# A hybrid attention and SwiGLU layer on one Trainium2 core: the last activation chunk transposed on TensorE, the first norm's Newton steps on VectorE, and masks given two more steps

## The chip, the cores and the metric

The program runs on one core of a Trainium2 chip. A core has TensorE (PE in the profile, its weight loads PEld), VectorE (DVE), ScalarE (ACT), GpSimd (POOL) and SyncE (SP, which here only issues transfers), and 16 DMA engines that all queues share. Each engine runs its own instructions in their written order and waits on semaphores for the others. The metric is the device time of one execution in microseconds. The time before is 1340.16 us, the median of three runs: 1338.07, 1340.16 and 1351.09.

## The reference

One layer over 256 positions of width 2048. Two matrices carry most of the weight traffic: the input projection (2048 x 12288) and the feed-forward pair (2048 x 11264 and 5632 x 2048). Cut to what matters here:

```python
def hybrid_layer(x, ...):
    h = rmsnorm(x, g_mix)                       # first norm
    proj = h @ w_in                             # q, k, v of 16 heads, and three gates of 2048
    gates = sigmoid(proj[..., 3 * MIX_WIDTH:])
    o_a = stick_breaking_attention(q, k, v)     # heads 0 to 3: masked, no softmax
    o_b = moba_attention(rmsnorm(q), rmsnorm(k), v, rel_bias)
    o_c = dilated_attention(rmsnorm(q), rmsnorm(k), v, rel_bias)
    merged = gates[0] * (o_a @ w_b[a]) + gates[1] * (o_b @ w_b[b]) + gates[2] * (o_c @ w_b[c])
    x = x + merged @ w_out
    gu = rmsnorm(x, g_ffn) @ w_gu               # second norm, then gate and up, 5632 columns each
    return x + (silu(gu[..., :D_FF]) * gu[..., D_FF:]) @ w_down
```

Stick-breaking attention weighs a key by exp(log sigmoid(z) + the sum of log sigmoid(-z) over the keys after it), and masks both factors to keys strictly before the query.

## The kernel before

**Tiling.** Every matmul is a 128 x 128 stationary block of weights times 512 moving columns. For accuracy each f32 operand is split in two f32r parts: ScalarE copies the high part (`w_hi`), VectorE subtracts it for the low part (`w_lo`), both on line 110 (`split`), and lines 181 to 183 (`product`) issue three matmuls: high by high, low by high, high by low. A pair of weight blocks (`[P, 2, 512]`, 512 KB) is fetched by SP, split in one ScalarE and one VectorE instruction of 128 x 1024, and then used by twelve matmuls in most places. Wide products use one level of Strassen's scheme on some chunks (`form`, `sums`), which saves matmuls and adds VectorE sums (`u`, L325, L336, L1152 to L1167).

**Stages.** First the input projection, unit by unit (`units`: v, gate, q and k, ...), with the attention of the finished heads woven in; then the branch products, the output product, the second norm, the gate-and-up product in eleven chunks of 512 columns (loop over `c`, L1047), and the down projection in two halves of 1024 columns (`down_pair`).

**What sets the order.** The program is written as generators that are advanced one step per weight pair: `stages` at each, `slow_stages` at every second (L310 to L318). A `yield` thus puts what follows one step later. `behind(n, step)` runs a step after the n-th split. From this a scheduler with a timeline of its own then fixes the order on each engine; instructions marked `keep_in_program_order` keep theirs. So a `yield` more or an instruction on another engine moves neighbours too.

**First norm.** The sum of squares (`sst`, L518) goes through `rsqrt_mean`: one multiply-add (L188), Ln and Exp on ScalarE (L190, L191), and two Newton steps of four small instructions each (L194 to L197), on GpSimd here. The result `rstd` scales the projection's rows, so it is applied when the accumulation banks are read: L786 copies the two banks of `v` (named `ps`), L772 the two of the first gate (named `qs`). The products that come next, of q and k, write into the same two `ps` banks.

**Masks.** `stick_breaking` handles two heads at a time. GpSimd masks the softplus values (`pT`, L559) and later the weights (`p`, L559); then come three `yield`s and the product with `v` (L652, L653).

**Activations.** After each of the eleven gate-and-up chunks ScalarE and VectorE form 2 x 128 x 512 activations `sg[t]` (L1053, L1054). They are needed transposed, with the feature on the partition. Each half `t` is turned by `turn_out` (a ScalarE copy of the 16-bit halves, L705, and a DMA transpose from ScalarE's queue, L707) and `turn_in` (a ScalarE copy back, L712), written to `a_mem` in HBM (L1040), and fetched again in the down projection (`fetch_a`, L1065; `take_a`), where it is split. Three chunks stay in the core (`EARLY`). The last chunk, c = 10, uses as room the two tiles that will later hold its own split (`a_hi`, `a_lo`), is turned while the down projection already runs, and is used last. The down projection also fetches weights through SP (L302, and L107 where the order is pinned); its third weight quarter `b21` (a `g_raw` tile) feeds the sum L1167.

Of the kernel before, what the change touches and what calls it, by code (L numbers as in the profile page):

```python
# [13 lines left out]
ALU = mybir.AluOpType  # L14
# [5 lines left out]
D = 2048  # L20
S = 256
NT = S // P
# [8 lines left out]
EPS = 1e-6  # L31
# [26 lines left out]
def hybrid_block(ctx: ExitStack, tc: tile.TileContext, x, rel_bias, w_in, w_branch, w_out, w_gu, w_down, xT, gains,  # L58
                 onehot, extra, out):
    nc = tc.nc  # L60
# [22 lines left out]
    def pool(stack, name, side, bufs=1):  # L83
        return stack.enter_context(tc.tile_pool(name=name, bufs=bufs, side=side, reuse_waits="tile"))
# [8 lines left out]
    def half_kb(dt=F32):  # L93

        return scratch.tile([P, NB], dt, name="sc")
# [23 lines left out]
    split_count = [0]  # L119
# [7 lines left out]
    def behind(n, step, *args):  # L127
        at_split.setdefault(n, []).append(lambda: step(*args))
# [53 lines left out]
        nc.tensor.matmul(ps, ah, wl, start=False, stop=False, **how)  # L182
        nc.tensor.matmul(ps, al, wh, start=False, stop=stop, **how)  # L183

    def rsqrt_mean(dst, ss, n, cols, engine=nc.vector):

        v = small.tile([P, cols], F32, name=f"rs_v{cols}")
        engine.tensor_scalar(v, ss, 1.0 / n, EPS, op0=ALU.mult, op1=ALU.add)  # L188
        y = small.tile([P, cols], F32, name=f"rs_y{cols}")
        nc.scalar.activation(y, v, AF.Ln)  # L190
        nc.scalar.activation(y, y, AF.Exp, scale=-0.5)  # L191
        t = small.tile([P, cols], F32, name=f"rs_t{cols}")
        for it in range(2):
            engine.tensor_mul(t, y, y)  # L194
            engine.tensor_mul(t, t, v)
            engine.tensor_scalar(t, t, -0.5, 1.5, op0=ALU.mult, op1=ALU.add)
            engine.tensor_mul(dst if it else y, y, t)  # L197

    def transpose4(src):

        pt = tr.tile([P, 4, P], F32, name="tr")
        for i in range(4):
            nc.tensor.transpose(pt[:, i, :], src[:, i * P:(i + 1) * P], ident)
        return pt
# [232 lines left out]
    def squares(xc, dst, c):  # L437
        for t in range(NT):
            nc.scalar.activation(half_kb(), xc[t], AF.Square, accum_out=dst[:, t, c:c + 1])

    ss1 = small.tile([P, NT, 4], F32, name="ss1", bufs=1)
    rstd = small.tile([P, NT], F32, name="rstd", bufs=1)
# [70 lines left out]
    def first_norm():  # L513
        for c in range(3, 4):
            squares(rows[c], ss1, c)
            yield
        sst = small.tile([P, NT], F32, name="sst", bufs=1)
        nc.vector.tensor_reduce(sst, ss1, op=ALU.add, axis=AX.X)  # L518
        rsqrt_mean(rstd, sst, D, NT, nc.gpsimd)
        yield  # L520

    rest = [rest_of_x()]
# [19 lines left out]
    def sums_of_h():  # L542
        yield
        yield
        for c in WC:
# [6 lines left out]
            yield  # L552

    stages.extend((*rest, first_norm()))
    slow_stages.append(sums_of_h())


    def keep_before(blk):
        nc.gpsimd.affine_select(out=blk, in_=blk, compare_op=ALU.is_gt, fill=0.0, base=0,  # L559
                                pattern=[[0, 2], [1, P]], channel_multiplier=-1)  # L560
# [42 lines left out]
    def diag_blocks(a):  # L603
        return (a[:, 0:W0].rearrange("p (h q) -> p h q", h=2)[:, :, 0:P],
                a[:, W0:W0 + W1].rearrange("p (h q) -> p h q", h=2))

    def finish(h0, po):
        nc.scalar.copy(o_raw[:, h0:h0 + 2, :], po)

    def stick_breaking(hl, qT, kT, v):  # L610
        z = att.tile([P, 2 * NB], F32, name="att")
        for i in range(2):
            nc.tensor.matmul(z[:, i * S:(i + 1) * S], kT[:, hl + i, 0:P], qT[:, hl + i, :], start=True, stop=True)
        for i in range(2):
            nc.tensor.matmul(z[:, W0 + i * P:W0 + (i + 1) * P], kT[:, hl + i, P:S], qT[:, hl + i, P:S],
                             start=True, stop=True)
        n = W0 + W1
        l = pa.tile([P, n], F32, name="p", bufs=1)
        nc.scalar.activation(l, z[:, :n], AF.Abs)
        nc.scalar.activation(l, l, AF.Exp, scale=-1.0)  # L620
        nc.scalar.activation(l, l, AF.Ln, bias=1.0)
        sp = pa.tile([P, n], F32, name="pT", bufs=1)
        sp_hi = pa.tile([P, n], F32R, name="sp_hi", bufs=1)
        lo = half_kb(F32R), pa.tile([P, W1], F32R, name="sp_lo", bufs=1)
        nc.vector.scalar_tensor_tensor(sp, z[:, :n], 0.0, l, op0=ALU.max, op1=ALU.add)
        lb = l
        nc.vector.scalar_tensor_tensor(lb, z[:, :n], 0.0, l, op0=ALU.min, op1=ALU.subtract)
        for blk in diag_blocks(sp):
            keep_before(blk)
        nc.scalar.copy(sp_hi, sp)  # L630
        for part, cols in zip(lo, (slice(0, W0), slice(W0, n))):
            nc.vector.tensor_sub(part, sp[:, cols], sp_hi[:, cols].bitcast(F32))
        yield
        yield
        yield
        c = att.tile([P, 2 * NB], F32, name="att")
        late = c[:, 0:W0].rearrange("p (h q) -> p h q", h=2)[:, :, P:S]
        for i, (early, part) in enumerate(((sp_hi[:, 0:W0], sp_hi[:, W0:n]), lo)):
            nc.tensor.matmul(c[:, 0:W0], neg_after, early, start=not i, stop=False, skip_group_check=True)
            nc.tensor.matmul(late, neg_ones, part.rearrange("p (h q) -> p h q", h=2), start=False, stop=bool(i), skip_group_check=True)  # L640
            nc.tensor.matmul(c[:, W0:n], neg_after, part, start=not i, stop=bool(i), skip_group_check=True)
        nc.vector.tensor_add(lb, lb, c[:, :n])
        nc.scalar.activation(lb, lb, AF.Exp)
        for blk in diag_blocks(lb):
            keep_before(blk)
        yield
        yield
        yield
        po = tr.tile([P, 2, S], F32, name="tr")
        for i in range(2):  # L650
            cols = slice((hl + i) * HD, (hl + i + 1) * HD)
            nc.tensor.matmul(po[:, i, :], v[:, 0, cols], lb[:, i * S:(i + 1) * S], start=True, stop=False)  # L652
            nc.tensor.matmul(po[:, i, P:S], v[:, 1, cols], lb[:, W0 + i * P:W0 + (i + 1) * P],  # L653
                             start=False, stop=True)
        finish(hl, po)
# [297 lines left out]
    def out_of_rows(src, rooms, pl, name, bufs):  # L953

        rooms.append(pl.tile([P, 2, NB], F32, name=name, bufs=bufs).rearrange("p k n -> p (k n)"))
        turn_out(src, rooms[-1])
# [38 lines left out]
    for c in range(4):  # L995
# [4 lines left out]
        if c == 0:  # L1000
# [3 lines left out]
            ORDER = [0, 1, 2, 4, 3, 6, 5, 8, 7, 9, 10]  # L1004
            EARLY = 3
            a = Chunks(None, "a", NF // 4, WD, False)
# [35 lines left out]
    def to_a(c, srcs, out_at, in_at, room):  # L1042
        n, rooms = split_count[0], []
        for t in range(NT):
            behind(n + out_at[t], lambda t: out_of_rows(srcs[t], rooms, *room(t)), t)
            behind(n + in_at[t], into_a, c, t, rooms)

    for c in range(D_FF // NB):
        nxt = (h2, w_gu, (c + 1) * NB, D_FF + (c + 1) * NB, True) if c + 1 < D_FF // NB else None
        (g0, g1_, u0, u1), ahead = project_pair(h2, w_gu, c * NB, D_FF + c * NB, ahead, nxt)  # L1050
        sg = [half_kb() for _ in range(NT)]
        for t, (g, u) in enumerate(((g0, u0), (g1_, u1))):
            nc.scalar.activation(sg[t], g, AF.Silu, scale=rstd2[:, t:t + 1])  # L1053
            nc.vector.scalar_tensor_tensor(sg[t], u, rstd2[:, t:t + 1], sg[t], op0=ALU.mult, op1=ALU.mult)  # L1054
        if c < 9:
            to_a(c, sg, (14, 18), (PAIR + 3, PAIR + 7), lambda t: (pr, "a_raw", 2))
        elif c == 9:
            to_a(c, sg, (6, 10), (14, 18), lambda t: (gd, "g_raw", 4))
        else:
            to_a(c, sg, (5, 9), (14, 18), lambda t: (pd, ("a_hi10", "a_lo10")[t], 1))  # L1060


    def fetch_a(c):
        raw = pr.tile([P, 2, NB], F32, name="a_raw", bufs=2).rearrange("p k (j q) -> p (k j) q", j=2)
        nc.sync.dma_start(raw, a_mem[c])  # L1065
        return raw
# [12 lines left out]
    pd = pool(ctx, "pd", "left")  # L1079

    def take_rest():
        cs = ORDER[EARLY:]
        raws = [fetch_a(c) for c in cs[:2]]
        for i, (c, steps) in enumerate(zip(cs, (4, 6, 5, 6, 6, 6, 7, 7))):
            for _ in range(steps):
                yield
            take_a(pd, c, raws.pop(0))
            if i + 2 < len(cs) - 1:
                raws.append(fetch_a(cs[i + 2]))
            elif i + 2 == len(cs):  # L1090
                for _ in range(0):
                    yield
                raws.append(fetch_a(cs[-1]))

    stages.append(take_rest())

    def more_sums(cs, rooms):
# [157 lines left out]
```

## Time and profile before

| | |
|---|---|
| Times of three runs | 1338.07, 1340.16, 1351.09 us |
| Profiled execution | 1350.9 us, its span 1349.2 us, mean granted clock 0.996 |
| PE / DVE / ACT / POOL busy | 1331.0 / 1202.8 / 945.5 / 58.8 us |
| HBM read, written | 303.66 MB, 12.60 MB |

Busy times are sums over instructions; PE's is modelled and full in almost every slice, so what counts is where it is not full, and where the clock that TensorE was granted is below 1.00. A row of the timeline gives start, length, engine, line, operation and tile names, and in brackets the idle time of that engine just before and who ended it. Line numbers are those of the kernel before.

### The profile page before, as it was taken

The page shows a single profiled execution, that of the slowest core. Times are in us where ns is not written, and L with a number is a line of the kernel's source. Part 1 is how long each engine was busy: PE and PEld are TensorE (multiplying, and loading weights), DVE is VectorE, ACT ScalarE, POOL GpSimd, SP SyncE. Part 2 cuts the span into 40 slices and gives each one's busy share as a digit, 9 for nine tenths or more (in the row PEclk, how much of TensorE's full clock was granted, in tenths as well). Part 3 has the DMA queues.
Part 4 walks back from the last instruction along what each step waited for, and adds up shares of the span by engine and source line. Part 5 has one row for each costly group of instructions (what it writes and reads, how often), then busy time and mean ns, then how long its engine had stood idle before and what let it go on. Part 6 is the DMA issues. An engine that isn't in the chain of part 4 may idle for free.

```text
span 1349.2 us, 17457 instructions
## 1 busy us (share of the span) xinstructions
PE 1331.0 (99%) x6194; PEld 1155.8 (86%) x6194; DVE 1202.8 (89%) x1272; ACT 945.5 (70%) x1209; POOL 58.8 (4%) x74
## 2 busy tenths in 40 slices
PE   9999999999999999999999999999999999899998
PEld 7788888888888888888878888888888888788887
DVE  6998998989889987774889999999999998799998
ACT  7777787788766766665757778787777776564563
POOL 0301100000110100000000000000000000000000
PEclk9999999999999999999999999999999999899999
DMA  9995768677888867999976767678878789878663
GB/s 349 302 286 167 232 194 254 218 235 206 259 253 250 280 184 249 284 274 205 272 252 235 240 207 239 209 218 263 261 243 257 237 249 238 297 256 274 223 216 107
DMA packets 206391, 326.33 MB, mean 242 GB/s; under 512 B 46776, under 2 KB 58576, under 8 KB 206304
## 3 DMA queue, kind: packets, MB, share of 16 engines
q1 hardware_dynamic: 151632, 291.54, 64.9%
q0 software_dynamic: 7872, 17.39, 6.2%
q10 hardware_dynamic: 46800, 16.29, 6.2%
q8 instruction: 48, 0.79, 0.2%
q14 instruction: 39, 0.32, 0.1%
HBM read 303.66 MB, written 12.60 MB: 234 GB/s over the span
## 4 chain that ended last, share of the span: by engine, by line
PE 43%; DMA 3%; DVE 2%; ACT 1%; issue 1%; SPq 0%; ACTq 0%; DVEq 0%
PE ps L181 4%; PE qs L182 4%; PE ps L182 4%; PE ps L183 4%; PE qs L183 4%; PE qs L181 4%; PE z L181 3%; PE z L182 3%; PE z L183 3%; PE v L181 2%; PE v L183 2%; PE v L182 2%; DVE w_lo L110 1%; PE tr L182 1%; PE tr L183 1%; PE tr L181 1%
## 5 line engine op out<-in xcount | busy, mean ns | idle before, releaser
L110 DVE TENSOR_TENSOR w_lo<-w_raw,w_hi 128x1024 fp32r<-128x1024 f32 x308 | 374.0, 1220 | 76.3 <-ACT w_hi L110 75.3
L110 ACT CAST w_hi<-w_raw 128x1024 fp32r<-128x1024 f32 x308 | 319.7, 1046 | 81.0 <-PE ps L183 20.4
L110 ACT CAST w_hi<-u 128x1024 fp32r<-128x1024 f32 x156 | 162.8, 1048 | 154.5 <-DVE u L325 85.1
L110 ACT CAST w_hi<-g_raw 128x1024 fp32r<-128x1024 f32 x208 | 214.8, 1048 | 72.1 <-PE ps L183 15.1
L110 DVE TENSOR_TENSOR w_lo<-g_raw,w_hi 128x1024 fp32r<-128x1024 f32 x208 | 247.7, 1218 | 12.9 <-ACT w_hi L110 11.6
L110 DVE TENSOR_TENSOR w_lo<-u,w_hi 128x1024 fp32r<-128x1024 f32 x156 | 186.3, 1220 | 18.7 <-ACT w_hi L110 18.2
L182 PE MATMUL ps<-w_lo,h_hi 128*128 128x512 f32 x328 | 125.7, 383 | 1.4 <-DVE w_lo L110 1.4
L183 PE MATMUL ps<-w_hi,h_lo 128*128 128x512 f32 x328 | 124.3, 379 | 0.0
L182 PE MATMUL qs<-w_lo,h_hi 128*128 128x512 f32 x316 | 120.5, 381 | 0.5 <-DVE w_lo L110 0.5
L183 PE MATMUL qs<-w_hi,h_lo 128*128 128x512 f32 x316 | 119.9, 379 | 0.0
L181 PE MATMUL ps<-w_hi,h_hi 128*128 128x512 f32 x328 | 118.5, 381 | 0.0
L181 PE MATMUL qs<-w_hi,h_hi 128*128 128x512 f32 x316 | 113.4, 381 | 0.3 <-ACT w_hi L110 0.3
L325 DVE TENSOR_TENSOR u<-u,g_raw 128x1024 f32<-128x1024 f32 x88 | 104.4, 1222 | 0.0
L182 PEld LDWEIGHTS ps<-w_lo,h_hi 128*128 128x128 f32 x328 | 62.0, 189 | 10.4 <-DVE w_lo L110 2.1
L183 PEld LDWEIGHTS ps<-w_hi,h_lo 128*128 128x128 f32 x328 | 62.0, 189 | 8.5
L181 PEld LDWEIGHTS ps<-w_hi,h_hi 128*128 128x128 f32 x328 | 61.8, 189 | 8.5
L182 PEld LDWEIGHTS qs<-w_lo,h_hi 128*128 128x128 f32 x316 | 59.8, 189 | 9.4 <-DVE w_lo L110 0.9
L181 PEld LDWEIGHTS qs<-w_hi,h_hi 128*128 128x128 f32 x316 | 59.7, 189 | 9.1 <-ACT w_hi L110 0.7
L183 PEld LDWEIGHTS qs<-w_hi,h_lo 128*128 128x128 f32 x316 | 59.8, 189 | 8.4 <-issue 0.2
L336 DVE TENSOR_TENSOR u<-g_raw 128x1024 f32<-128x1024 f32 x44 | 53.7, 1221 | 3.4 <-DMA g_raw<-in_w_gu 3.4
L181 PE MATMUL v<-w_hi,h_hi 128*128 128x512 f32 x112 | 43.4, 388 | 0.0
L181 PE MATMUL z<-w_hi,h_hi 128*128 128x512 f32 x112 | 42.8, 382 | 0.2 <-ACT sc L320 0.2
(427 smaller groups left out, 2962.3 us busy)
## 6 DMA issues: line engine op xcount, KB each, us to landing
w_raw<-in_w_in SPq DMA_DIRECT2D x100, 512.0 KB, 5.7
g_raw<-in_w_in SPq DMA_DIRECT2D x88, 512.0 KB, 5.6
g_raw<-in_w_gu SPq DMA_DIRECT2D x88, 512.0 KB, 5.4
w_raw<-in_w_gu SPq DMA_DIRECT2D x88, 512.0 KB, 5.8
w_raw<-in_w_down SPq DMA_DIRECT2D x56, 512.0 KB, 5.5
w_raw<-in_w_branch SPq DMA_DIRECT2D x32, 512.0 KB, 4.9
w_raw<-in_w_out SPq DMA_DIRECT2D x32, 512.0 KB, 5.8
g_raw<-in_w_down SPq DMA_DIRECT2D x32, 512.0 KB, 5.6
```

What stands on the lines that cost most here:

```text
L110: for op in nc.scalar.copy(hi, src), nc.vector.tensor_sub(lo, src, hi.bitcast(F32)):
L181: nc.tensor.matmul(ps, ah, wh, start=start, stop=False, **how)
L182: nc.tensor.matmul(ps, ah, wl, start=False, stop=False, **how)
L183: nc.tensor.matmul(ps, al, wh, start=False, stop=stop, **how)
L325: tc.keep_in_program_order(nc.vector.tensor_add(d, d, a))
L336: nc.vector.tensor_add(d, a, b)
```

## The change

Four edits. (1) `rsqrt_mean` loses its engine argument: the first norm's nine small instructions go from GpSimd to VectorE. (2) Before the product with `v` in `stick_breaking` stand five `yield`s for three. (3) The last activation chunk (c = 10) is placed in its final tiles at once, and after the third, fourth split of the down projection each half is transposed by four TensorE instructions into a PSUM tile (`transpose4`, L200) and split from there; its two DMA transposes, four 16-bit copies, two writes to `a_mem`, one fetch and one 128 x 1024 split are gone. (4) `take_rest` therefore ends one chunk earlier.

```diff
-    def rsqrt_mean(dst, ss, n, cols, engine=nc.vector):
+    def rsqrt_mean(dst, ss, n, cols):
...
-        engine.tensor_scalar(v, ss, 1.0 / n, EPS, op0=ALU.mult, op1=ALU.add)
+        nc.vector.tensor_scalar(v, ss, 1.0 / n, EPS, op0=ALU.mult, op1=ALU.add)
...
-            engine.tensor_mul(t, y, y)
+            nc.vector.tensor_mul(t, y, y)
...
-        rsqrt_mean(rstd, sst, D, NT, nc.gpsimd)
+        rsqrt_mean(rstd, sst, D, NT)
...
         for blk in diag_blocks(lb):
             keep_before(blk)
-        yield
-        yield
-        yield
+        for _ in range(5):
+            yield
         po = tr.tile([P, 2, S], F32, name="tr")
...
         else:
-            to_a(c, sg, (5, 9), (14, 18), lambda t: (pd, ("a_hi10", "a_lo10")[t], 1))
+            behind(split_count[0] + 3, lambda: a.place(pd, c))
+            for t in range(NT):
+                behind(split_count[0] + 3 + t, lambda t: a.put(c, t, transpose4(sg[t])), t)
...
     def take_rest():
-        cs = ORDER[EARLY:]
+        cs = ORDER[EARLY:-1]
         raws = [fetch_a(c) for c in cs[:2]]
         for i, (c, steps) in enumerate(zip(cs, (4, 6, 5, 6, 6, 6, 7, 7))):
             for _ in range(steps):
                 yield
             take_a(pd, c, raws.pop(0))
-            if i + 2 < len(cs) - 1:
+            if i + 2 < len(cs):
                 raws.append(fetch_a(cs[i + 2]))
-            elif i + 2 == len(cs):
-                for _ in range(0):
-                    yield
-                raws.append(fetch_a(cs[-1]))
```

Three places show how the scheduler's order answers. VectorE at the first norm, before (`o_raw` holds the first activations, `u` is a Strassen sum of two weight tiles, `sst` here is the scaled copy of `rstd`):

```order
L110 TENSOR_TENSOR w_lo<-w_raw,w_hi 128x1024
L224 TENSOR_TENSOR o_raw<-o_raw 128x2x128
L110 TENSOR_TENSOR w_lo<-w_raw,w_hi 128x1024
L229 TENSOR_TENSOR o_raw<-o_raw 128x2x128
L110 TENSOR_TENSOR sc<-sc 32x12
L814 TENSOR_SCALAR sst<-rstd 128x2
L110 TENSOR_TENSOR w_lo<-g_raw,w_hi 128x1024
L227 TENSOR_TENSOR o_raw<-o_raw 128x2x128
L336 TENSOR_TENSOR u<-g_raw 128x1024
```

Here no Newton step stands on VectorE, and `rstd` comes from GpSimd ahead of the first `w_lo<-g_raw`. VectorE at the same place now, from the third Newton instruction on:

```order
L110 TENSOR_TENSOR b_slo_101<-o_raw,b_shi_100 128x1024
L336 TENSOR_TENSOR u<-g_raw 128x1024
L228 TENSOR_TENSOR o_raw<-o_raw 128x2x128
L197 TENSOR_TENSOR rs_y_436<-rs_y_436,rs_t_439 128x2
L589 TENSOR_TENSOR sc<-sc,tr 12x384
L110 TENSOR_TENSOR w_lo<-g_raw,w_hi 128x1024 x2
L110 TENSOR_TENSOR w_lo<-u,w_hi 128x1024
L229 TENSOR_TENSOR o_raw<-o_raw 128x2x128
L194 TENSOR_TENSOR rs_t_439<-rs_y_436 128x2
L195 TENSOR_TENSOR rs_t_439<-rs_t_439,rs_v_434 128x2
L196 TENSOR_SCALAR rs_t_439<-rs_t_439 128x2
L197 TENSOR_TENSOR rstd<-rs_y_436,rs_t_439 128x2
```

`rstd` (the last row) now comes after the splits and sums of the next unit: nine 1024-wide instructions stand between the first Newton instruction and it, five of them in these rows.

TensorE where the first gate ends and the q and k product begins, before (`qs_139` and `qs_140` are the gate's banks, `ps_597` is the first bank of q and k, the same memory as the first bank of `v`; `w_hi_538` is the gate's last weight pair, `w_hi_564` the first of q and k):

```order
L181 MATMUL qs_140<-w_hi_538,h_hi_98 128x512
L181 MATMUL ps_597<-w_hi_564,h_hi_98 128x512
L182 MATMUL qs_139<-w_lo_539,h_hi_98 128x512
L183 MATMUL qs_139<-w_hi_538,h_lo_99 128x512
L182 MATMUL qs_140<-w_lo_539,h_hi_98 128x512
L588 MATMUL tr_498<-sc_474,sc_475 12x384
L183 MATMUL qs_140<-w_hi_538,h_lo_99 128x512
L181 MATMUL qs_139<-w_hi_538,h_hi_98 128x512
```

One product of q and k stands ahead of the last ten of the gate. The same place now:

```order
L183 MATMUL qs_139<-w_hi_538,h_lo_99 128x512
L181 MATMUL qs_140<-w_hi_538,h_hi_98 128x512
L182 MATMUL qs_140<-w_lo_539,h_hi_98 128x512
L183 MATMUL qs_140<-w_hi_538,h_lo_99 128x512
L181 MATMUL ps_597<-w_hi_564,h_hi_98 128x512
L182 MATMUL ps_597<-w_lo_565,h_hi_98 128x512
L183 MATMUL ps_597<-w_hi_564,h_lo_99 128x512
L181 MATMUL ps_597<-w_hi_564,h_hi_98 128x512
L182 MATMUL ps_597<-w_lo_565,h_hi_98 128x512
```

All of the gate's products come first, and then nothing but products into the banks of `v`.

ScalarE at the head of the down projection, before (`a_shi` is a Strassen sum's high part, `u` a weight sum):

```order
L110 CAST w_hi<-g_raw 128x1024
L110 CAST a_shi_10133<-a_raw 128x1024
L705 COPY a_hi_10151<-sc 128x1024
L110 CAST w_hi<-w_raw 128x1024
L705 COPY a_lo_10224<-sc 128x1024
L707 DMA_TRANSPOSE a_hi_10151<-a_hi_10151 128x8x128
L707 DMA_TRANSPOSE a_lo_10224<-a_lo_10224 128x8x128
L110 CAST w_hi<-u 128x1024
L110 CAST w_hi<-w_raw 128x1024
L110 CAST a_hi_10259<-a_raw 128x1024
```

The same place now:

```order
L110 CAST w_hi<-g_raw 128x1024
L110 CAST a_hi_10097<-tr 128x4x128 x2
L110 CAST a_shi_10149<-a_raw 128x1024
L110 CAST w_hi<-w_raw 128x1024
L110 CAST w_hi<-u 128x1024
L110 CAST w_hi<-w_raw 128x1024
L110 CAST a_hi_10269<-a_raw 128x1024
L110 CAST w_hi<-u 128x1024
```

Two 128 x 512 casts out of PSUM stand for the two 16-bit copies and two DMA transposes; the later copies back and the writes to `a_mem` are gone too. On TensorE the eight transposes stand 48 matmuls ahead of the first product into `z`. Between the middle of the attention and this place, 3474 of the 6140 TensorE rows in a row are the same in both kernels, and so is nearly all that follows.

## Rows read from the trace of the kernel before

**Rows 1.** Busy time by stage: us, PE, PEld, DVE, ACT, POOL busy (instructions), PEclk granted clock, DMA, GB/s

```profile
45.00:60.00 15.00, 12.84 (x56) 9.85 (x55) 14.54 (x16) 13.66 (x16) 4.26 (x5) 1.00 0.90 286
...
600.00:615.00 15.00, 14.35 (x67) 12.24 (x65) 7.16 (x8) 8.29 (x9) 0.00 (x0) 1.00 0.89 191
615.00:630.00 15.00, 14.18 (x64) 12.13 (x65) 9.01 (x10) 9.85 (x15) 0.00 (x0) 1.00 0.77 241
...
690.00:705.00 15.00, 12.72 (x56) 9.99 (x55) 14.22 (x24) 8.96 (x15) 0.00 (x0) 0.93 0.49 160
705.00:720.00 15.00, 14.49 (x64) 12.26 (x64) 12.76 (x12) 9.74 (x11) 0.00 (x0) 0.96 0.61 207
...
1140.00:1155.00 15.00, 11.42 (x54) 9.68 (x52) 8.63 (x9) 10.99 (x13) 0.00 (x0) 0.95 1.09 300
1155.00:1170.00 15.00, 15.00 (x58) 12.66 (x59) 14.93 (x18) 7.00 (x8) 0.00 (x0) 0.82 0.93 312
```

**Rows 2.** Timeline of GpSimd and ScalarE at the first norm: start, length, instruction

```profile
38.91 3.72 POOL L584 CAST sc<-sc 32x384 fp32r<-32x384 f32 x1
...
44.48 1.27 ACT L786 ACTIVATE v<-ps,rstd 128x512 f32<-128x512 f32 x2 [3.50 <-POOL rstd L197]
```

**Rows 3.** Timeline of TensorE around the end of the first gate

```profile
48.50 0.38 PE L182 MATMUL ps<-w_lo,h_hi 128*128 128x512 f32 x1
...
52.63 0.48 PE L182 MATMUL ps<-w_lo,h_hi 128*128 128x512 f32 x1 [1.39 <-DVE w_lo L110]
```

**Rows 4.** Timeline of VectorE at the first norm

```profile
39.24 1.21 DVE L110 TENSOR_TENSOR w_lo<-w_raw,w_hi 128x1024 fp32r<-128x1024 f32 x1
40.37 0.41 DVE L224 TENSOR_TENSOR o_raw<-o_raw 128x256 f32<-128x256 f32 x1
40.71 1.21 DVE L110 TENSOR_TENSOR w_lo<-w_raw,w_hi 128x1024 fp32r<-128x1024 f32 x1
```

**Rows 5.** Timeline of VectorE in a later norm, whose Newton steps it does

```profile
158.60 0.17 DVE L196 TENSOR_SCALAR rs_t<-rs_t 128x16 f32<-128x16 f32 x1
158.80 0.17 DVE L197 TENSOR_TENSOR rs_y<-rs_y,rs_t 128x16 f32<-128x16 f32 x1
```

**Rows 6.** Waits of TensorE, whole span: in total, times, longest (us)

```profile
PE tr L652 <- POOL p L559: 1.0, 1, 1.0
```

**Rows 7.** Timeline of TensorE: eight transposes of the same shape in the attention

```profile
95.49 1.04 PE L203 MATMUL tr<-ident,sc 128*128 128x128 f32 x8
96.28 0.46 PE L182 MATMUL ps<-w_lo,b_shi 128*128 128x512 f32 x1
```

**Rows 8.** Timeline of TensorE at the head of the down projection

```profile
1143.14 0.38 PE L181 MATMUL v<-w_hi,a_shi 128*128 128x512 f32 x1
...
1150.91 0.38 PE L181 MATMUL tr<-w_hi,a_shi 128*128 128x512 f32 x1
1154.87 0.79 PE L182 MATMUL tr<-w_lo,a_shi 128*128 128x512 f32 x1 [3.58 <-DVE w_lo L110]
...
1160.42 0.38 PE L183 MATMUL ps<-w_hi,a_lo 128*128 128x512 f32 x1
```

**Rows 9.** Timeline of VectorE at the head of the down projection

```profile
1152.46 1.22 DVE L1167 TENSOR_TENSOR u<-u,g_raw 128x1024 f32<-128x1024 f32 x1 [6.33 <-DMA g_raw<-in_w_down]
```

**Rows 10.** The chain that ended last, in order of time: start, length, what

```profile
669.14 11.46 DMA sc<-in_x
680.61 6.84 DMA w_raw<-in_w_gu
...
1137.94 14.43 DMA g_raw<-in_w_down
```

**Rows 11.** DMA queues from 1138 to 1142 us: packets, MB, share of the 16 engines

```profile
q10 hardware_dynamic: 1147, 0.29, 63.1%
q1 hardware_dynamic: 118, 0.41, 35.4%
```

**Rows 12.** The page's DMA issues: count, KB each, median us from issue to landing

```profile
g_raw<-in_w_down SPq DMA_DIRECT2D x32, 512.0 KB, 5.6
```

More of the change, by code (lines that the diff above doesn't have):

```diff
@@ L193, in rsqrt_mean @@
         for it in range(2):
-            engine.tensor_mul(t, y, y)
-            engine.tensor_mul(t, t, v)
-            engine.tensor_scalar(t, t, -0.5, 1.5, op0=ALU.mult, op1=ALU.add)
-            engine.tensor_mul(dst if it else y, y, t)
+            nc.vector.tensor_mul(t, y, y)
+            nc.vector.tensor_mul(t, t, v)
+            nc.vector.tensor_scalar(t, t, -0.5, 1.5, op0=ALU.mult, op1=ALU.add)
+            nc.vector.tensor_mul(dst if it else y, y, t)
     def transpose4(src):
```

## The prediction, made before the change was run

> **What bounds the kernel.** I read the busy time by stage first, to find where TensorE is not full or not at its high clock; then the waits of TensorE and the chain of waits, to see what each such place waited for; then the timeline of each engine there. Nearly everywhere TensorE runs back to back: between 1143.14 and 1150.91 us stand 36 matmul steps [rows 8], 0.216 us each, and no other engine can shorten that. So only its gaps count. In [rows 1] the reader sees three kinds: 2.2 us idle at 45 to 60 us; idle and a clock below 1.00 from 690 to 720; and 3.6 us idle at 1140 to 1155 with the clock at 0.82 in the next 15 us. Between these the two kernels' TensorE orders are the same for 3474 rows, so the change can act only before some 390 us and after 1125 us.
>
> **Part by part, against the profiled execution (1350.9 us).**
>
> *Newton steps on VectorE.* Before, GpSimd made `rstd`, held up by a 3.72 us cast, and ScalarE, which waited for it until 44.48 us, then freed the two banks of `v`, 1.27 us for both [rows 2]. TensorE lost nothing to that, it was still in the gate. Now the steps stand in VectorE's queue between weight splits. I add up that queue from the split that starts at 39.24 us [rows 4]; the steps ahead of it put it at 39.3. From there to `rstd` stand ten 1024-wide instructions at 1.13 from start to start [rows 4]: 11.3; five 256-wide sums at 0.34 [rows 4]: 1.7; two small ones that I put at 0.4 each, an estimate from the 256-wide ones: 0.8; four lone Newton instructions at some 0.1, since one that waits for none of its kind fills only its slot: 0.4; the last four, each waiting for the one before, at 0.20 [rows 5]: 0.8. Together 15.0, so `rstd` comes at 54.3 us, ten later. Behind it on ScalarE stand the copies of both `v` banks, a table load, the gate's two reads and the next splits; the first copy ends 0.64 later (half of 1.27), so a bank is free at 55.0. TensorE has finished the gate at about 48.3: the row that follows the gate before starts at 48.50 [rows 3] and one product of q and k that stood earlier is gone. In the new order nothing but products into the `v` banks follows, so it waits 48.3 + 0.2 to 55.0: 6.5 us. The splits that those products need are done by then, so the 2.2 us that it waited here before [rows 1, 3] are contained in it. Net +4.3. Then the clock. After a gap of 3.58 us the 13 steps from 1154.87 to 1160.42 took 5.55 us for 2.8 [rows 8], 2.7 lost at the low level of 1.2 GHz; around 690 to 720 the granted 0.93 and 0.96 [rows 1] mean 2 x (0.07 + 0.04) x 15 = 3.3 us at that level, 1.65 lost; after the 1.39 us gap [rows 3] the clock stayed at 1.00. A gap of 6.5 us is nearest the longest of these, but one that ends in uninterrupted work can do with the shorter loss: 1.65 to 2.7, I take 2.4. **+6.7**, at least +3 (a walk 1.3 us shorter and no fall of the clock), at most +7.5.
>
> *Masks.* The product with `v` waited 1.0 us for the second pair's mask [rows 6]. Two steps later the mask is long done. What is late next is the projection's own splits, which stand as they did. **-1.0**, between -1.3 and 0. The attention behind it is reordered; that is a rival below.
>
> *TensorE transposes.* Eight took 0.79 us from their start to the next matmul's, and that one ran 0.08 longer [rows 7]: **+0.9**, all on the path, since TensorE is full there. The two casts and two subtractions of 128 x 512 take the place of copies and a split that were longer; ScalarE and VectorE do no more than before in sum. ScalarE's queue loses four transfers and SP's one; nothing is moved past another. The Trainium skill ("TensorE: Matmul & The Clock Gate", Part 4: PE-mode transpose) gives about 275 ns for one such transpose inside a kernel. By that figure the term would be an estimate of 2.2 instead of 0.9; the trace has eight overlapping [rows 7], so the measured 0.9 stands.
>
> *DMA transposes gone.* This is the gain. The third weight quarter of the first Strassen chunk was issued at 1137.94 and landed 14.43 us later [rows 10], where such a load takes 5.6 [rows 12]. In the four middle microseconds ScalarE's queue (q10, the two transposes) held 63.1% of the DMA engines for 0.29 MB, SP's queue (q1) 35.4% for 0.41 MB [rows 11]. VectorE, in order, stood on that load for 6.33 us with every later split behind it [rows 9], and TensorE ran dry. With 5.6 us the load lands at 1143.6, before VectorE asks for it at 1146.1 (1152.46 less 6.33), so the whole loss goes: from 1150.91 to 1160.42 stand 14 steps, 3.0 us of work in 9.5 [rows 8], **-6.5**. If the load still came late, 0. The removed fetch and writes were on no one's path.
>
> *Sum on the profiled execution:* 6.7 - 1.0 + 0.9 - 6.5 = +0.1.
>
> **From the profiled execution to the median.** It is 10.7 us above the median of 1340.16, and one of the three runs, 1351.09, is like it. What can a run lack that this one has? TensorE's work is the same in each, and the wait for `rstd` or the mask comes from the order. What varies is the landing of transfers. There are three such losses here: 6.5 in the down projection; 2.28 + 0.51 idle and 1.65 clock at 690 to 720 [rows 1], where the chain shows transfers of 11.46 and 6.84 us [rows 10]; and 0.65 + 0.82 at 600 to 630 [rows 1], which I count as a transfer's too. Together 6.5 + 4.4 + 1.5 = 12.4. To be 10.7 faster the median run must lack most of them, so it keeps 1.7 of 12.4, about 0.9 of the 6.5. The gain in the median is then 0.9, while the loss at the norm comes in full: 1340.2 + 6.7 - 1.0 + 0.9 - 0.9 = **1345.9**, 0.4% more.
>
> About 1% (13.4 us, the spread of the three runs) is what a measurement of this kernel tells from no change.
>
> **The rivals.**
>
> *The late load is in every run, and is cured.* For it: the transposes stand at the same place in each run. Against it: the 10.7 us above. 1340.2 + 0.1 = 1340.3.
>
> *A short wait for `rstd`.* With the lower bound +3 and the clock kept: 1340.2 + 3 - 1.0 + 0.9 - 0.9 = 1342.2, or 1336.6 with the late load cured in every run. For it: the walk adds rows of one execution. Against it: VectorE's queue is in order and each term is measured.
>
> *Taking the transposes away does not help the loads.* Then they wait for bytes alone: 0.52 MB less, at the 300 GB/s of that stage [rows 1] 1.7 us, so a gap of 3.6 shrinks to 1.9 and the clock may still fall: 1340.2 + 6.7 - 1.0 + 0.9 - 1.7 = 1345.1 if every run has the gap, and its middle stays visible in the trace. The Trainium skill says it so ("Advanced Engine Details and Errata", X-Bar Transpose (TRN2)): transpose DMAs are as fast as regular ones. The trace differs: 63.1% of the engines for 41% of the bytes [rows 11].
>
> *Slower: the attention's chain comes too late.* The first four transposes of the normalised q and k of the second group of heads stand at TensorE's row 740 before and 799 now, 59 rows or 12.7 us later. If the scores, softmax and the product with `v` that hang on them have less slack than that before the next group needs their tiles, TensorE waits up to 12.7: 1345.9 + 12.7 = 1358.6, 1.4% slower. For it: it is the largest move in the order. Against it: before, 160 rows (34.5 us) lie between that group's last product (row 888) and row 1048, from which the orders agree again.
>
> **How the numbers follow.** Forecast 1345.9: 0.44. Load cured in every run: 0.27. Short wait: 0.12. No help for the loads: 0.09. Late attention: 0.08. The range leaves out the last, and takes in the lower bound of the second rival (1336.6) and, above, the term at its most (+7.5, no masks' gain: 1347.7) plus a median that falls among runs like the 1351.09: 1337 to 1353. Faster by over 1% means under 1326.8, which no case reaches: 0.02. Slower means over 1353.6: the attention's 0.08 and a little for such runs: 0.09. Within 1%: 0.89.
>
> **What the profile after would show.** `rstd` on VectorE near 54 us; ScalarE's first `v` copy waiting for it; TensorE idle some 6.5 us from about 48.5, and a granted clock of 0.50 for two to five microseconds after 55. No wait at L652 of the order of 1 us. The transposes some 0.9 us long at about 1129. The quarter's load landing in about 6 us, VectorE not waiting for it, clock 1.00 from 1140 to 1170. I am wrong at the norm if TensorE resumes before 52 us, and on the gain if the gap at 1150 stays, or if it was in every run and the median falls to 1340.

## The result, and the profile after

The changed kernel took 1348.41 us, the median of 20 runs (1344.75 to 1357.93); the kernel before, timed beside it, 1341.82 us, the median of 20 (1334.43 to 1351.09). The ratio is 1.0058, 95% interval 1.0038 to 1.0078: +7.8 us, between 5.1 and 10.5. Forecast were 1345.9 us and "within 1%". The profiled execution took 1346.3 us (span 1344.5, clock 0.997), and lies 2.1 below the median. Its line numbers are one lower than before from the attention on, and three lower in the down projection. The forecast's range, 1337 to 1353, also holds a kernel that did not change at all, so it is the profile that has to bear out the reasons.

Stage by stage (span, busy us of PE, PEld, DVE, ACT, POOL with counts, granted clock, DMA share, GB/s), beside [rows 1]:

```profile
45.00:60.00 15.00, 8.57 (x27) 6.39 (x27) 10.13 (x18) 9.87 (x11) 4.24 (x5) 0.78 1.03 294
600.00:615.00 15.00, 15.00 (x72) 13.12 (x71) 11.02 (x13) 9.97 (x11) 0.00 (x0) 1.00 0.87 264
615.00:630.00 15.00, 15.00 (x71) 13.15 (x70) 9.48 (x10) 10.92 (x13) 0.00 (x0) 1.00 0.66 200
690.00:705.00 15.00, 14.78 (x73) 12.65 (x72) 13.81 (x24) 10.33 (x17) 0.00 (x0) 1.00 0.44 152
705.00:720.00 15.00, 14.49 (x68) 12.37 (x67) 14.40 (x14) 10.16 (x11) 0.00 (x0) 1.00 0.65 220
1140.00:1155.00 15.00, 15.00 (x71) 13.15 (x70) 14.93 (x16) 11.43 (x13) 0.00 (x0) 1.00 0.93 317
1155.00:1170.00 15.00, 15.00 (x71) 13.12 (x71) 14.97 (x16) 7.88 (x8) 0.00 (x0) 1.00 0.91 316
```

One stretch became much worse: at 45 to 60 us TensorE is busy 8.57 us instead of 12.84, at a clock of 0.78. All that was lost at 600 to 630 and 1140 to 1170 is gone, and most of the loss at 690 to 720; at 600 to 720 both kernels have the same order on TensorE, so that part is not the change's doing but differs from one execution to the next (last experiment). The first norm on TensorE (start, length, instruction, and in brackets the idle time before it and who ended it), where [rows 3] stood:

```profile
48.09 0.38 PE L183 MATMUL qs<-w_hi,h_lo 128*128 128x512 f32 x1
54.89 0.79 PE L181 MATMUL ps<-w_hi,h_hi 128*128 128x512 f32 x1 [6.43 <-ACT v L785]
55.48 0.63 PE L182 MATMUL ps<-w_lo,h_hi 128*128 128x512 f32 x1
...
60.17 0.43 PE L181 MATMUL ps<-w_hi,h_hi 128*128 128x512 f32 x1
```

TensorE stands for 6.43 us until a bank of `v` is copied out, and then does 12 steps from 54.89 to 60.17, 0.44 each where [rows 8] have 0.216: the lower clock level. That level had set in during the gap already (same columns as above):

```profile
53.00:53.40 0.40, 0.00 (x0) 0.00 (x0) 0.37 (x3) 0.20 (x1) 0.00 (x0) 1.00 0.93 280
53.40:54.00 0.60, 0.00 (x0) 0.00 (x0) 0.50 (x4) 0.60 (x1) 0.00 (x0) 0.53 0.87 250
```

VectorE and ScalarE in the same stretch, answering [rows 2, 4]:

```profile
53.68 0.16 DVE L197 TENSOR_TENSOR rstd<-rs_y,rs_t 128x2 f32<-128x2 f32 x1
```

```profile
53.20 1.04 ACT L110 CAST b_shi<-o_raw 128x1024 fp32r<-128x1024 f32 x1 [3.62 <-DVE o_raw L229]
54.16 1.26 ACT L785 ACTIVATE v<-ps,rstd 128x512 f32<-128x512 f32 x2
```

`rstd` is done at 53.8 (before: 44.4), and the copy of `v` starts at 54.16, behind a cast that waited 3.62 us for VectorE as well. Since the copy needs `rstd` too, that cast can have cost it no more than 0.3 us. In the down projection the eight transposes (answering [rows 7]), the sum that had waited for the third quarter [rows 9], the queues from 1138 to 1142 us [rows 11] and the quarters' transfers:

```profile
1128.92 1.04 PE L203 MATMUL tr<-ident,sc 128*128 128x128 f32 x8
1129.71 0.46 PE L181 MATMUL qs<-w_hi,a_hi 128*128 128x512 f32 x1
```

```profile
1147.70 1.22 DVE L1164 TENSOR_TENSOR u<-u,g_raw 128x1024 f32<-128x1024 f32 x1
```

```profile
q1 hardware_dynamic: 383, 0.99, 77.6%
```

```profile
g_raw<-in_w_down SPq DMA_DIRECT2D x5, 512.0 KB, 5.4
```

The transposes take 0.79 + 0.08 us, the sum has no bracket, so it waits for nothing, q10 moves nothing there, and the quarters land in 5.4 us (median from 1125 to 1160 us). Last, TensorE's waits from 60 to 330 us, where [rows 6] had the mask:

```profile
PE qs L182 <- DVE w_lo L110: 0.8, 1, 0.8
PE ps L182 <- DVE w_lo L110: 0.8, 1, 0.8
PE qs L181 <- ACT sc L816: 0.7, 1, 0.7
PE qs L181 <- ACT w_hi L110: 0.2, 1, 0.2
```

The mask's wait of 1.0 is gone, and others stand there.

### The profile page after: what moved, and what is told of

The parts are those of the page before. It is cut to its first block, busy times and chain, and to the rows that moved or that the text cites. A ratio compares the mean times of both kernels' runs of the same rounds, so it can differ in the third digit from the quotient of the medians.

```text
span 1344.5 us, 17466 instructions
## 1 busy us (share of the span) xinstructions
PE 1329.3 (99%) x6202; PEld 1155.3 (86%) x6202; DVE 1203.7 (90%) x1282; ACT 942.7 (70%) x1206; POOL 51.5 (4%) x65
## 4 chain that ended last, share of the span: by engine, by line
PE 84%; DVE 6%; ACT 3%; DMA 3%; issue 2%; SPq 0%; DVEq 0%; ACTq 0%; POOLq 0%
PE ps L182 10%; PE ps L183 10%; PE ps L181 10%; PE qs L182 10%; PE qs L183 10%; PE qs L181 10%; PE z L181 4%; PE z L183 4%; PE z L182 4%; DVE w_lo L110 3%; PE v L181 2%; PE v L183 2%; PE v L182 2%; ACT w_hi L110 2%; DMA w_raw<-in_w_down 1%
## 5 line engine op out<-in xcount | busy, mean ns | idle before, releaser
L182 PE MATMUL v<-w_lo,h_hi 128*128 128x512 f32 x112 | 42.4, 379 | 0.0
```

## The experiments

My theory: the loss is TensorE's wait for `rstd` and the clock behind it; the other edits come to nothing in a median run, since that run hardly has the late load. Rivals: the late load is in every run (A); the norm costs half of that and the attention's order the rest (B); the transposes' removal does not help the loads (C); VectorE is too full for the steps wherever they stand (D). Times below are medians of 12 runs unless said otherwise; the kernel before, beside them, 1340.92 us (32 runs) for the steps back on GpSimd, the steps alone, the steps held together and the transposes alone, and 1341.64 (29 runs) for the others. "Lost" is the distance between two matmuls' starts less the 0.216 us of a step.

### Newton steps back on GpSimd, masks and transposes kept

```diff
-        rsqrt_mean(rstd, sst, D, NT)
+        rsqrt_mean(rstd, sst, D, NT, nc.gpsimd)
```

> The changed kernel with the first norm's nine small instructions back on GpSimd; the masks' two more steps and the TensorE transposes stay. My theory (the whole loss is TensorE's wait for rstd, +6.7, and the other edits come to about -1 in a median run): 1.005 times faster than the changed kernel, about 1341 us, TensorE's wait for the copy of v near 55 us gone and its clock at 1.00 from 45 to 60 us. Rival A (the late load in the down projection is in every run of the kernel before, and is cured): about 1335. Rival B (the attention's new order costs, the norm only some 3 us): about 1345.

1343.07 us, ratio 1.0011 (0.9987 to 1.0035), or +1.5 us (-1.7 to +4.7). The loss is gone, A's 1335 is below the interval (1339.2 to 1345.6), B's 1345 within it. There is no wait for `v`, and the clock is 1.00 from 45 to 60 us.

### Newton steps on VectorE alone

```diff
-        rsqrt_mean(rstd, sst, D, NT, nc.gpsimd)
+        rsqrt_mean(rstd, sst, D, NT)
```

> The kernel before with only the first norm's small instructions moved to VectorE (the order on TensorE differs from the kernel before in 115 lines, all around the norm). My theory: +6.7 us, ratio 1.005, a wait of about 6.5 us for the copy of v and 2 to 3 us lost at the low clock behind it. Rival B (a short wait, no clock): +3 us, ratio 1.002. If the norm alone comes to +8 or more, the rest of the change is worth nothing.

1349.20 us, ratio 1.0062 (1.0042 to 1.0081): +8.3 us, between 5.6 and 10.9. This edit alone is as slow as all four, which leaves B's +3 outside. By the sign named above, +8 or more, the rest of the change is worth nothing. TensorE's timeline:

```profile
48.29 0.38 PE L183 MATMUL qs<-w_hi,h_lo 128*128 128x512 f32 x1
54.96 0.79 PE L181 MATMUL ps<-w_hi,h_hi 128*128 128x512 f32 x1 [6.29 <-ACT v L786]
...
58.11 0.45 PE L182 MATMUL ps<-w_lo,h_hi 128*128 128x512 f32 x1
```

The same wait; 6.45 are lost in it, and 1.6 in the seven slow steps to 58.11 (3.15 less 7 x 0.216). The kernel before loses 1.54 + 0.47 + 0.62 = 2.6 here to late splits, so this execution, the fastest of its twelve, lost 5.5 more than it. That is just below the interval of the times; what the slower runs lost beyond it no trace here shows.

### Only one of the two Newton steps on VectorE

```diff
...
-        for it in range(2):
+        for it in range(2 - steps, 2):
...
-        rsqrt_mean(rstd, sst, D, NT, nc.gpsimd)
+        rsqrt_mean(rstd, sst, D, NT, steps=1)
```

> The kernel before with the first norm's small instructions on VectorE and only one of its two Newton steps (the second step of that norm is left out). The queue is the same up to the first step's end, so rstd comes at about 49.0 us instead of 53.7. My theory (the loss follows rstd's place in VectorE's queue): the copies of v start at 49.5, behind a cast, TensorE waits about 1.9 us from 48.3 instead of 6.3, the clock stays at 1.00, and with the late splits of the kernel before still to come the time is 0 to 2 us above that kernel's, ratio 1.000 to 1.0015. Rival B' (the loss comes from taking VectorE's time or from the order around the attention): still +6 to +8, ratio 1.005 or more.

1341.16 us, ratio 0.9999 (0.9982 to 1.0015): the whole loss is gone when four small instructions are left out. `rstd` on VectorE, the copies on ScalarE, and TensorE:

```profile
49.70 0.14 DVE L197 TENSOR_TENSOR rstd<-rs_y,rs_t 128x2 f32<-128x2 f32 x1
```

```profile
50.31 1.26 ACT L786 ACTIVATE v<-ps,rstd 128x512 f32<-128x512 f32 x2
```

```profile
48.90 0.38 PE L183 MATMUL qs<-w_hi,h_lo 128*128 128x512 f32 x1
51.04 0.48 PE L181 MATMUL ps<-w_hi,h_hi 128*128 128x512 f32 x1 [1.77 <-ACT v L786]
51.36 0.38 PE L182 MATMUL ps<-w_lo,h_hi 128*128 128x512 f32 x1
```

`rstd` comes four microseconds earlier, TensorE waits 1.77 instead of 6.29, and goes on at full speed. What it loses here, 1.92 + 0.36 + 0.73 = 3.0, is close to the 2.6 of the kernel before. TensorE's order is the same in this kernel and the one above until 55 us, so the order there is not what costs, and neither is the engine: it is how late `rstd` comes in VectorE's queue. One thing moved along with it: ScalarE's `b_shi` cast, which stood ahead of the copies, now stands behind them. By the 0.3 us above, it is a small part.

### The changed kernel with its Newton steps held together

```diff
...
-            nc.vector.tensor_mul(t, y, y)
+            keep(nc.vector.tensor_mul(t, y, y))
...
-        rsqrt_mean(rstd, sst, D, NT)
+        kept_splits[:] = ['low'] * 2; rsqrt_mean(rstd, sst, D, NT, tc.keep_in_program_order)
```

`keep` holds an instruction in its written order, and `kept_splits` does so for VectorE's half of the next two weight splits.

> The changed kernel with the Newton steps on VectorE as there, but the eight held together: they and the next two weight splits keep their written order, so no 1024-wide instruction stands between the first step and rstd. The Exp that they start from ends at 37.5 us in the changed kernel. My theory (what costs is the place in VectorE's queue, not the engine): rstd near 39.5 us, no wait of TensorE for the copy of v, at most 2 us lost because VectorE idles for the Exp; 1341 to 1343 us, ratio to the changed kernel 0.995. Rival D (VectorE is too full there to take the steps at all, the splits become late instead): as slow as the changed kernel, with TensorE waiting for w_lo for 5 us or more between 40 and 60 us.

1346.39 us (9 runs), ratio 1.0036 (1.0019 to 1.0054): better than the changed kernel's 1.0058, though the intervals overlap, and short of what I expected. VectorE and TensorE:

```profile
37.04 0.15 DVE L194 TENSOR_TENSOR rs_t<-rs_y 128x2 f32<-128x2 f32 x1
...
38.42 0.16 DVE L197 TENSOR_TENSOR rstd<-rs_y,rs_t 128x2 f32<-128x2 f32 x1
38.50 1.23 DVE L110 TENSOR_TENSOR w_lo<-w_raw,w_hi 128x1024 fp32r<-128x1024 f32 x1
```

```profile
37.66 0.59 PE L181 MATMUL qs<-w_hi,h_hi 128*128 128x512 f32 x2
39.78 0.48 PE L182 MATMUL qs<-w_lo,h_hi 128*128 128x512 f32 x1 [1.52 <-DVE w_lo L110]
```

`rstd` comes at 38.4, and no wait for `v` is left. But a weight split now stands behind the chain, and TensorE waits 1.52 for it. From 34 to 64 us this kernel loses 0.37 + 1.69 + 0.96 + 0.51 + 0.89 = 4.4, which is 1.8 more than before. D is right in this much: early steps push splits back.

### The masks' edit alone, with five steps and with four

```diff
-        yield
-        yield
-        yield
+        for _ in range(5):
+            yield
```

> The kernel before with only the masks' edit: five steps instead of three ahead of the masked product with v. My prediction said -1.0 us (ratio 0.999). The traces of the two kernels above that hold this edit say otherwise, which is now my theory: TensorE loses 1.04 at the mask no more, but 0.7 to a scaled copy near 145 us and twice 0.8 to late weight splits near 153 and 236 us, in sum about 1 more than before: +1 us, ratio 1.001. If the prediction's term was right: ratio below 1.000 and none of those three waits.

1343.01 us, ratio 1.0014 (0.9997 to 1.0030). No gain; whether it is a small loss the times leave open. The trace has the three new waits. One of the two longest, on TensorE, and ScalarE ahead of it:

```profile
150.96 0.48 PE L181 MATMUL ps<-w_hi,b_shi 128*128 128x512 f32 x1
152.22 0.48 PE L182 MATMUL ps<-w_lo,b_shi 128*128 128x512 f32 x1 [0.78 <-DVE w_lo L110]
```

```profile
149.87 1.04 ACT L110 CAST w_hi<-u 128x1024 fp32r<-128x1024 f32 x1
```

Both queues in the kernel before (its second profile, the last experiment):

```profile
153.17 0.46 PE L181 MATMUL ps<-w_hi,b_shi 128*128 128x512 f32 x1
```

```profile
150.05 1.99 ACT L110 CAST w_hi<-u 128x1024 fp32r<-128x1024 f32 x2
```

ScalarE casts this weight sum at nearly the same time in both, after a block of sums of squares for the norm of q and k (L723, from 144.69 to 149.78 without a gap, one copy among them). TensorE used to come to it at 153.17, since it had waited for the mask and done masked products first. With five steps no masked product stands there any more; TensorE comes to it at 150.96, and waits for the weight instead. Up to 126 us the second profile lags by 0.8 us, so TensorE comes 1.4 us earlier by this edit, and ScalarE's cast 0.6 later.

From 120 to 330 us five steps lose 0.18 + 0.74 + 0.30 + 1.04 + 0.18 + 0.26 + 1.04 = 3.7, three steps in the first profile 0.43 + 1.30 + 0.18 + 0.67 = 2.6: +1.1. In the second profile the 0.43 is missing, which makes it +1.5.

With `range(4)` in place of `range(5)`:

> The kernel before with four steps instead of three ahead of the masked product. Theory (what the five steps cost comes from the reordering that follows, not from the number of steps): the mask is done a step later too, so the 1.04 us wait is gone, and whether others take its place is a matter of the order: between -2 and +1 us, and the three waits of the five-step version need not be there. Rival (any delay of the masked product makes the next splits late): the same waits of 0.7 to 0.8 us as with five steps, +1 us.

1340.69 us, ratio 1.0002 (0.9985 to 1.0019). The mask's wait is gone, one of the three others too, and one is shorter (0.42):

```profile
PE ps L182 <- DVE w_lo L110: 0.8, 1, 0.8
PE qs L181 <- ACT sc L816: 0.4, 1, 0.4
```

In sum 2.3 are lost from 120 to 330 us, 0.3 less than in the first profile. The rival expected all three waits again, which the trace does not show. No time here tells four steps from three.

This execution shows something else, at the first norm. VectorE where it takes `rstd` from GpSimd, in the first profile of the kernel before and here:

```profile
44.48 0.17 DVE L814 TENSOR_SCALAR sst<-rstd 128x2 f32<-128x2 f32 x1 [1.82 <-POOL rstd L197]
```

```profile
42.69 0.17 DVE L813 TENSOR_SCALAR sst<-rstd 128x2 f32<-128x2 f32 x1 [0.30 <-POOL rstd L197]
```

The order of TensorE, VectorE and ScalarE is the same up to 70 us, but in this execution GpSimd was done 1.8 us earlier (why is not shown), and TensorE's wait of 1.39 us for a split [rows 3] is absent. In the kernel before, too, TensorE thus lost time behind a late `rstd`.

### The transposes alone

```diff
-            to_a(c, sg, (5, 9), (14, 18), lambda t: (pd, ("a_hi10", "a_lo10")[t], 1))
+            behind(split_count[0] + 3, lambda: a.place(pd, c))
+            for t in range(NT):
+                behind(split_count[0] + 3 + t, lambda t: a.put(c, t, transpose4(sg[t])), t)
...
```

> The kernel before with only the last activation chunk transposed on TensorE (Newton steps on GpSimd, three steps before the masked product as before). My theory: a median run of the kernel before has hardly any of the 6.5 us that its profiled execution lost to the late load, so +0.9 for the eight transposes and -0.9 for the load: no change, ratio 1.000 within 0.001. Rival A (the late load is in every run, and cured): -5.6 us, ratio 0.996. Rival C (the removal does not help the loads): +0.9 us, ratio 1.001, and the gap near 1150 us stays in the trace.

1342.11 us, ratio 1.0016 (0.9995 to 1.0037). A's 0.996 is outside; my 1.000 and C's 1.001 are both inside. The trace has no gap near 1150, against C, which wanted one. In the kernel with Newton steps alone, whose down projection has no gap, the last matmul starts 256.2 us after the tenth chunk's first Silu; in the four executions with TensorE transposes it starts 257.1 to 258.2 us after it: 0.9 to 2.1 more, of which 0.87 is the transposes' own.

### The kernel before, once more

> The kernel before once more, unchanged, for a second profile of it. My theory (a median run hardly has the transfer losses of the first profile): no gap near 1150 us, 1140 to 1170 at clock 1.00, and a time near 1340. Rival A (the late load is in every run): a gap of some 3.6 us near 1150 again.

1338.01 us in one run. By stage, and TensorE at the place of [rows 8]:

```profile
1140.00:1155.00 15.00, 14.62 (x68) 12.47 (x67) 13.19 (x17) 11.28 (x13) 0.00 (x0) 1.00 1.06 402
1155.00:1170.00 15.00, 15.00 (x71) 13.14 (x70) 13.78 (x13) 8.87 (x12) 0.00 (x0) 1.00 0.71 250
```

```profile
1144.32 0.48 PE L182 MATMUL tr<-w_lo,a_shi 128*128 128x512 f32 x1 [0.39 <-DVE w_lo L110]
```

The gap of 3.58 us is one of 0.39 here, at full clock. For the same matmuls the first profile takes 8.1 us longer between 600 and 720 us and 5.8 longer between 1140 and 1170. The spans differ by 12.9 (1349.2 and 1336.3), so these two stretches account for all of it; this execution loses 1.1 more elsewhere, most of it before 34 us. Over the ten profiled executions the loss between 600 and 720 us runs from about 1 to about 9. Altogether six executions that still have the DMA transposes were profiled; they lose 6.5, 0.5, 0, 0, 0 and 1.6 at this place (1.4 on average). The four without them lose nothing there, but so do three of the six.

## Why the prediction was right, and where it was not

**What bounds it: right.** Wherever the kernels differ in time, TensorE has a gap, the lower clock or the eight transposes; elsewhere its 512-column steps take 0.216 us in all of them.

**Newton steps on VectorE, +6.7: right in size and mechanism.** `rstd` was put at 54.3, and was done at 53.8; the wait was put at 6.5, and was 6.43; the clock's loss was put at 2.4, and was 2.7 here and 1.6 in the other execution. The first `v` copy came behind a cast as well as behind `rstd`; both wait for VectorE. One step was wrong: "TensorE lost nothing to that" does not hold for the kernel before, as the execution with four mask steps shows; the size was not touched by it, since the 2.2 us waited there were taken off. The edit alone was timed at +8.3 (5.6 to 10.9), which holds the 6.7. That it is a place in a queue, and not an engine, is shown by the single Newton step (`rstd` 4 us earlier, and the loss is gone) and by the steps held together (all eight on VectorE, and no wait for `v`). The rival of a short wait falls.

**Masks, -1.0: wrong in sign.** The wait of [rows 6] went as forecast. The step that failed is "What is late next is the projection's own splits, which stand as they did": they do not. The reordering, which I set down as a rival and priced by TensorE's rows, brings TensorE 1.4 us earlier to a weight pair that ScalarE casts no earlier than before. The traces say +1.1 to +1.5, the times +1.9 (-0.4 to +4.0). I had not walked ScalarE's queue there.

**TensorE transposes, +0.9: right.** 0.87. In the down projection up to 1.2 more was lost, most of it in small waits (in the changed kernel 0.37 at 1123, 0.28 at 1202 and 0.21 at 1207 us), which I had not foreseen; with the steps held together there were none, so they may belong to the execution and not to the edit.

**DMA transposes gone, -6.5 in the profiled execution, -0.9 in the median: right as far as the traces tell.** The load that was late in one profile is on time in the next one of the same kernel, so the gain is mostly a piece of one execution's luck. The six losses average 1.4, their median lies below 0.5; no time here resolves 0.9. The argument that held was the subtraction: an execution 10.7 above the median must have losses that the median lacks.

**No help for the loads** falls in part. The Trainium skill ("Advanced Engine Details and Errata", X-Bar Transpose (TRN2)) calls such transposes as fast as regular DMAs. In the six executions that have them a 256 KB transpose landed in 6.5 to 11.9 us, a 512 KB quarter in 6.4 to 10.4 (medians); in the four without, quarters took 5.4 to 7.2. The two plain 256 KB writes that the same queue makes later landed in 7.4 to 9.0, so by landing times of one size the trace does not disagree. By engine time it does. The queue's share in the second profile, over the 11.7 us of the two transposes and over the 14.0 us of the two writes:

```profile
q10 hardware_dynamic: 2112, 0.52, 27.9%
```

```profile
q10 hardware_dynamic: 1056, 0.52, 12.4%
```

That is 52 us of the 16 engines' time against 28 for the same bytes; in the other five executions the transposes held 41 to 77. Other transfers ran beside both, and no run measured a transpose by itself.

**Late attention, +12.7:** did not happen as priced; its small form is the masks' +1.1 to +1.5.

**The sum.** At the norm the changed kernel's profile lost 9.27, or 6.6 more than the 2.63 before, and the profile of the steps alone 5.5 more. With 1.1 to 1.5 for the masks, 0.9 for the transposes, 0 to 1.2 for the small waits behind them, and less 0.3 to 1.4 for the late load, this gives 6.1 to 9.9 for a typical run; measured were 7.8 (5.1 to 10.5). The same terms without the norm give 0.6 to 3.3 for the steps back on GpSimd (measured 1.5, between -1.7 and 4.7), and with 1.8 at the norm 2.4 to 5.1 for the steps held together (measured 4.8, between 2.5 and 7.2). My 5.7 lay inside, 2 too low. The masks' sign alone accounts for that much, but the times are too coarse to say that nothing else took part. No version here beats the kernel before: the five whose interval holds 1 are one Newton step on VectorE (0.9999, and it leaves out a step), four mask steps (1.0002), steps on GpSimd with both other edits (1.0011), five mask steps (1.0014) and the transposes (1.0016).

## What to carry to other kernels

A small instruction moved onto a busy in-order engine costs what stands ahead of it there, for everyone who waits on its result: walk that queue to the consumer, and give the wait its clock loss too. When an edit moves a step in time, walk every engine's queue there, not only the one whose wait it removes. And before a stall of one profile is booked as a gain, ask how that execution stands to the median: a second profile of the same kernel shows which gaps belong to the program and which to the run.

## What the runs showed of the hardware that I had not expected

The same pair of waits near 700 us (0.73 to 0.74 us, one step, 1.31 us) was followed by a granted clock at the lower level in two executions (the first of the kernel before, and five mask steps alone) and by none in three (steps back on GpSimd, four mask steps, one Newton step). The executions were not alike ahead of the pair: from 660 us on, the two had lost 2.0 and 2.9 us, the three 1.9, 1.3 and 1.4; what decides stays open. Behind the 6.3 and 6.4 us gaps at the norm stood 7 and 12 slow steps, 3.2 and 5.3 us. The level had fallen at different points of the two gaps, at 51.4 us in the one and 53.4 in the other, and rose again at 58.2 and 60.2; so a gap of the same length cost 1.6 or 2.7 us, by where in it the clock fell. After 1.77 us in the same place it never fell. And one unchanged program on one core spreads from 1334.4 to 1351.1 us, and the 12.9 us between two of its executions lie in the stretches where the first profile's chain of waits holds late transfers [rows 10].
